# A hybrid decoder block on one core: raw weight places, retention's order and up's first sums

## The chip, the core and the metric

The kernel runs on one core of a Trainium2 chip. The core has a matrix engine (TensorE, here PE, with its weight loads as PEld), a vector engine (VectorE, DVE), a scalar engine (ScalarE, ACT), GpSimd (POOL) and SyncE (SP), which issues most transfers between the chip's memory and the core's own (SBUF). Products land in eight PSUM banks of 128 x 512 numbers. The engines run side by side, each through its own list of instructions in order, and wait for one another by semaphores. The metric is the device time of one launch in microseconds (us).

## What is computed

A decoder block over 1024 tokens of width 1024, in fp32. Cut to what matters here:

```
xn = rmsnorm(x, norm1_g)
qa, ka, va, qr, kr, vr, gr, gate_a, gate_b = split(xn @ w_in)     # w_in: 1024 x 12800
o_a = mix over three groups of dilated windowed attention (12 heads of 128, chunks of 128)
o_r = head_groupnorm(retention(qr, kr, vr)) * silu(gr)            # 4 heads, 8 chunks of 128
y = sigmoid(gate_a) * (o_a @ w_proj_a) + sigmoid(gate_b) * (o_r @ w_proj_b)
x = x + y @ w_out
x = x + square(relu(rmsnorm(x, norm2_g) @ w_up)) @ w_down         # 4096 wide
```

Retention goes over a head's chunks in order: a chunk's output is its decayed scores times its values, plus its queries times a state of 256 x 512, which each chunk then updates.

## The kernel before

**Products.** Every fp32 number is split into a high and a low half that PE takes (`split`: ACT copies the high half, DVE subtracts it). One product is then three matmuls of 128 x 512, high by high, high by low and low by high (`Pipe.group`, matmul at L271). Weights (`Weights`, called W) come as raw tiles of 128 x 1024 numbers into a few *raw places*, are split at L367 (ACT) and L370 (DVE) into places of their own, and a raw place may be loaded anew once its tile is split. Places raw0 to raw2 are there always, raw3 in a pool `more`, raw4 and raw5 in a pool `most` that is open only in some stages. Several stages use Strassen's scheme with seven products for eight: sums of weight quarters are made in the raw places by DVE (L122 for the token units, L158 for the units of up) before they are split. Pieces of a unit are named A, B, C and D, and `W` works its list of pieces in order: a piece waits for its target's earlier use to be freed, and for its raw tile.

**Stages, by time.** Norm and attention's inputs to about 400 us; then the gates, retention's queries and keys, and gr (units "in"), with attention's blocks put between its 168 steps, to about 951. Attention's three groups are mixed in four parts per pass (loads into a tile `edge`, weights L482 to L495, mix L498 and L500 on DVE, then four transposes at L506 on PE). Then the token units of retention's values (rv) to 1120; retention itself, to about 1443, laid over *fill steps* of projection a (16 of 12 matmuls) and projection b (first steps, 16 of 24 matmuls, and second steps, 8); the last second steps; out (16 rows of 24 matmuls) from about 1490; up from about 1579; down from about 1900 to 2216.

**Pools.** In the "in" stage the pools sgp (tiles `sg` for gate and gr outputs), pu0 and att lie on one stack, all closed after the stage; then `most2` opens at their place, for raw4 and raw5. So the first loads into raw4 and raw5 there come behind whatever still uses that memory, the stores `sr_d<-sg` of gr (L873) among it.

**Retention's rounds.** There are 32 items (4 heads of 8 chunks) and a round for each, plus two at the end. In round m the acts are, in this order: `turn_o(m-2)` (transposes at L1105 of the normed output `on`, scale on ACT at L1109, times the gate `sr` at L1111, split), `output(m-1)` (chunk's output, ACT copy L1068, statistics on DVE L1070 to L1072, a power on POOL L1073, norm L1075), `update(m-1)` (two products into the state, L1089 and L1091), `prepare(m)` (splits of the state into `Sh` and `Sl`) and `decay(m)` (scores L1028, mask L1030, their splits, keys turned). Acts are spread over the groups of a fill step. `share` says how many fill steps a round has: ten rounds share the 16 of projection a. Scores, output and the two updates of a round take turns in three PSUM banks, "ms".

**Projection b.** A first step puts its sum into memory (`pb_d`, tile `t`, ACT at L980); a second step loads it back (`begin`, L985 on, load at L940), ACT puts it into a PSUM bank (L992), and PE adds the second half of the terms on it.

**Out and up.** In out's second half each row is normed (sum of squares on ACT, power on POOL L384, scale on DVE L1242) and turned (`turn_xn`, L1178 to L1198), one to two rows later, with up's sums of activations made on the way. The raw tiles of up's unit 0 and 1 are loaded in out's stage; `w_out`'s last tiles use the weight places 4, 5, 2 and 3, and place 4 is up's place for piece D.

The order of PE's instructions is as written; on the other engines a scheduler sets it from the program's dependences and its own estimates.

Of the kernel before, what the change touches and what calls it, by code (L numbers as in the profile page):

```python
# [10 lines left out]
F = mybir.dt.float32  # L11
R = mybir.dt.float32r
# [25 lines left out]
class Weights:  # L38
# [93 lines left out]
    def add_units(self, tag, srcs):  # L132
# [7 lines left out]
        def piece(key, buf, r, cols, then=None, after=(), pinned=False):  # L140
            def step():
                if isinstance(buf, tuple):
                    if not kept:
                        kept["D"] = self.buffer(buf[0])
                    h, l = (x[:, 512 * buf[1]:512 * buf[1] + 512] for x in kept["D"])
                else:
                    h, l = self.buffer(buf)
                self.split(h, l, self.raw[r][:, cols], pinned)
                self.units[key] = h, l
                if then:  # L150
                    then()

            self.steps.append((self.claim(buf, key).union(after), r, step))
# [7 lines left out]
        for j in range(-1, len(srcs)):  # L161
            if j + 1 < len(srcs):
                r = base + 2 * (j + 1)
                piece((tag, j + 1, "A"), self.A[(j + 1) % 2], r, both,
                      after=((tag, j, "A"),) if j > 0 else (), pinned=tag == "up" and j > 0)
            if j >= 0:
                r = base + 2 * j
                piece((tag, j, "D"), (self.D, j % 2), r + 1, slice(0, 512), lambda r=r: sums(r))
# [149 lines left out]
def hybrid_block(ctx: ExitStack, tc: tile.TileContext, a: dict, out: bass.AP):  # L318
# [87 lines left out]
    for nb in range(2):  # L406
        for u in range(4):
            W.add(a["w_out"][nb, u], (4, 5, 2, 3)[u] if nb else (2, 3, 0, 1)[u])
# [8 lines left out]
    def product(tag, j, name, unit, operands, pu, result):  # L417
# [24 lines left out]
        elif name == "N5":  # L442
            u["u3"] = pu().tile([P, 512], F, name="u3")
            nc.scalar.activation(u["u3"], ps, AF.Copy)
        elif name == "N7":
# [300 lines left out]
    est, gates_ = ExitStack(), ExitStack()  # L746
# [3 lines left out]
    def open_gates():  # L750

        nonlocal sgp, pu, att, cmb, dist
        assert not pipe.due
        tok.close()
        W.most = None
        cmb = pool(est, "cmb", 1).tile([P, 2608], F, name="edge")
        sgp = pool(gates_, "sgp", 2)
        pu = pool(gates_, "pu0", 2)
        att = pool(gates_, "att", 2)
# [80 lines left out]
    def begins(n):  # L840
        return 3 + (n * 19) // 12
# [5 lines left out]

    def begin_mix(s, i):
        nonlocal mixing
        mixing = combine(s, i, cmb, joined.pop((s, i)))  # L850
# [7 lines left out]
    with ExitStack() as ph:  # L858

        def result(j, f, cs, src):  # L860
# [12 lines left out]
            nc.sync.dma_start(sr_d[2 * (n - NQ) + f, :, cs] if n >= NQ else rqk_d[n // 2, n % 2, f, :, cs], sg)  # L873
# [13 lines left out]
    tok = ExitStack()  # L887
    W.most = pool(tok, "most2", 1)
    W.pump()
# [42 lines left out]
    with ExitStack() as ph:  # L932
# [41 lines left out]

        def first_step(n):
            d, cs = n % KT, (lo, hi)[n // KT]
            pp = mm.tile([P, 512], F, name="mm")
            project(d, (inner, before)[n // KT], pp, True)
            t = pm2.tile([P, 512], F, name="t")
            nc.scalar.activation(t, pp, AF.Copy)  # L980
            nc.sync.dma_start(pb_d[d, :, cs], t)

        begun = {}

        def begin(n):  # L985

            if n < 2 * KT and n not in begun:
                d, cs = n % KT, (lo, hi)[n // KT]
                t = loaded(pm2, pb_d[d, :, cs], "t")
# [18 lines left out]
        share = [2, 1, 2, 1, 2, 2, 1, 2, 1, 2] + [1] * 24  # L1008
# [4 lines left out]
        def load_sr(m):  # L1013
            if m < len(ITEMS):
                h, c = ITEMS[m]
                srs[m] = p2.tile([P, 4, P], F, name="sr", bufs=3)
                nc.sync.dma_start(srs[m], sr_d[4 * h:4 * h + 4, :, c * P:(c + 1) * P].rearrange("f p t -> p f t"))

        def decay(m):
# [9 lines left out]
            sm = p2.tile([P, 2, P], F, name="sm", bufs=1)  # L1029
# [26 lines left out]
        def output(m):  # L1056
# [10 lines left out]
            on = it["o"] = p2.tile([P, DV], F, name="on")  # L1067
# [46 lines left out]
        for m in range(2):  # L1114
            load_sr(m)
        for m in range(len(ITEMS) + 2):
            acts = []
            if m >= 2:
                acts.append(lambda m=m: turn_o(m - 2))
            if 1 <= m <= len(ITEMS):  # L1120
                acts += [lambda m=m: output(m - 1), lambda m=m: update(m - 1)]
            if m < len(ITEMS):
                load_item(m + 2)
                load_sr(m + 2)
# [4 lines left out]
                acts += [lambda m=m: prepare(m), lambda m=m: decay(m)]  # L1129
# [32 lines left out]
    with ExitStack() as ph:  # L1162
# [4 lines left out]
        ssq = cp.tile([P, NT, 4], F, name="ssq")  # L1167
        kept = {}
# [4 lines left out]
        def turn_xn(xn, t, q):  # L1173

            pt = tr.tile([P, 4, P], F, name="tr")
# [320 lines left out]
```

## Time and profile before

| | |
|---|---|
| time, median of 3 runs | 2222.08 us (2219.28 to 2225.76) |
| the profiled execution | 2218.63 us |
| its span | 2216.5 us |
| PE busy | 2156.0 us, 97% |
| DVE busy | 1488.6 us, 67% |
| ACT busy | 1141.5 us, 51% |
| POOL busy | 163.6 us, 7% |
| moved by DMA | 403.28 MB, mean 182 GB/s |

The span is the time from the first to the last recorded instruction. In rows of the timeline stand the start, the length, the engine, the line, the operation, and its tiles (out<-in, numbers left out); brackets give the idle time before it and what ended it. In rows of waits stand the total idle time, its number and the longest. In rows on transfers stand the count, the KB of each, and the median time from issue to landing.

### The profile page before, as it was taken

To read this page: it belongs to the slowest core of one execution; us is meant where nothing else is said; L and a number is where in the kernel's file an instruction comes from. 1 tells how busy PE (TensorE), PEld (TensorE's weight loads), DVE (VectorE), ACT (ScalarE), POOL (GpSimd) and SP (SyncE) were. 2 spreads that over 40 slices of the span, in tenths; PEclk is the share of its full clock that TensorE was granted. 3 is DMA by queue.
4 is the path that set the end of the run, shared out by engine and by line. 5 is a ranking of instruction groups with operands and counts; after the bars stand their busy time and mean duration, and the time that the engine had idled before them with its cause. 6 is when DMAs were issued, how large, how long until landed. Compare 5 with 4: busy or idle time off the path is not lost.

```text
span 2216.5 us, 28593 instructions
## 1 busy us (share of the span) xinstructions
PE 2156.0 (97%) x9968; PEld 1770.1 (80%) x9968; DVE 1488.6 (67%) x2627; ACT 1141.5 (51%) x1990; POOL 163.6 (7%) x175
## 2 busy tenths in 40 slices
PE   8999999999999999979999999999899999999998
PEld 6888788888888887868877887888688888778887
DVE  8767676454656666656579777763877878686863
ACT  6434453577844477732246666542677777532210
POOL 1114343000000000000000000100000000000002
PEclk9999999999999999989999999999999999999999
DMA  6434434454555545444577555674378889976758
GB/s 201 129 114 115 152 85 122 152 165 138 172 155 157 174 149 158 147 138 143 171 237 224 181 162 148 175 243 140 98 222 248 248 251 281 325 280 229 258 216 176
DMA packets 336482, 403.28 MB, mean 182 GB/s; under 512 B 35345, under 2 KB 252049, under 8 KB 336338
## 3 DMA queue, kind: packets, MB, share of 16 engines
q1 hardware_dynamic: 332642, 394.38, 56.6%
q0 software_dynamic: 3696, 7.08, 2.1%
q8 instruction: 79, 1.29, 0.2%
q14 instruction: 65, 0.53, 0.1%
HBM read 262.87 MB, written 138.51 MB: 181 GB/s over the span
## 4 chain that ended last, share of the span: by engine, by line
PE 60%; issue 29%; DVE 4%; ACT 3%; DMA 3%; POOL 1%; SPq 0%; POOLq 0%; ACTq 0%; DVEq 0%
PE mm L271 30%; PE ms L271 24%; PE tr L808 1%; PE tr L827 1%; PE tr L661 1%; PE tr L820 1%; DVE wl L370 1%; PE tr L1105 1%; PE ms L1028 1%; DVE xl L370 1%; POOL out L1338 1%; DMA sr_d<-sg 0%; ACT L814 0%; ACT L868 0%; ACT wh L367 0%
## 5 line engine op out<-in xcount | busy, mean ns | idle before, releaser
L367 ACT ACTIVATE wh<-raw 128x1024 fp32r<-128x1024 f32 (+1 forms) x320 | 317.5, 994 | 320.6 <-PE ms L271 187.3
L370 DVE TENSOR_TENSOR wl<-raw,wh 128x1024 fp32r<-128x1024 f32 (+1 forms) x320 | 367.6, 1153 | 148.2 <-ACT wh L367 145.3
L271 PE MATMUL mm<-xh,wh 128*128 128x512 f32 x960 | 398.6, 415 | 5.5 <-ACT mm L992 4.0
L271 PE MATMUL mm<-xl,wh 128*128 128x512 f32 x960 | 376.4, 392 | 1.7 <-DVE xl L370 1.7
L271 PE MATMUL mm<-xh,wl 128*128 128x512 f32 x960 | 377.1, 393 | 0.5 <-DVE wl L370 0.5
L271 PEld LDWEIGHTS mm<-xh,wl 128*128 128x128 f32 x960 | 180.6, 188 | 40.4 <-DVE wl L370 1.0
L271 PEld LDWEIGHTS mm<-xh,wh 128*128 128x128 f32 x960 | 181.5, 189 | 38.9 <-ACT mm L992 4.4
L271 PE MATMUL mm<-wh,xh 128*128 128x512 f32 x528 | 208.8, 395 | 0.0
L271 PEld LDWEIGHTS mm<-xl,wh 128*128 128x128 f32 x960 | 181.6, 189 | 32.6 <-DVE xl L370 2.4
L271 PE MATMUL mm<-wh,xl 128*128 128x512 f32 x528 | 206.1, 390 | 1.5 <-DMA xl<-h_d 1.5
L271 PE MATMUL mm<-wl,xh 128*128 128x512 f32 x528 | 205.8, 390 | 0.0
L271 PE MATMUL ms<-wh,xh 128*128 128x512 f32 x512 | 205.3, 401 | 0.3 <-ACT wh L367 0.3
L271 PE MATMUL ms<-xh,wh 128*128 128x512 f32 x480 | 200.7, 418 | 0.6 <-ACT u L441 0.6
L271 PE MATMUL ms<-wl,xh 128*128 128x512 f32 x512 | 200.3, 391 | 0.9 <-DVE ss L383 0.8
L271 PE MATMUL ms<-wh,xl 128*128 128x512 f32 x512 | 200.6, 392 | 0.0
L271 PE MATMUL ms<-xl,wh 128*128 128x512 f32 x480 | 187.9, 391 | 0.7 <-DVE xl L370 0.7
L271 PE MATMUL ms<-xh,wl 128*128 128x512 f32 x480 | 188.1, 392 | 0.0
L271 PEld LDWEIGHTS mm<-wh,xl 128*128 128x128 f32 x528 | 99.3, 188 | 22.9 <-DMA xl<-h_d 1.9
L271 PEld LDWEIGHTS mm<-wh,xh 128*128 128x128 f32 x528 | 99.4, 188 | 19.7 <-ACT ms L1327 0.4
L271 PEld LDWEIGHTS mm<-wl,xh 128*128 128x128 f32 x528 | 99.4, 188 | 19.5
L271 PEld LDWEIGHTS ms<-wl,xh 128*128 128x128 f32 x512 | 96.9, 189 | 20.8 <-DVE wl L370 1.9
L271 PEld LDWEIGHTS ms<-wh,xl 128*128 128x128 f32 x512 | 96.6, 189 | 21.1
(304 smaller groups left out, 3806.5 us busy)
## 6 DMA issues: line engine op xcount, KB each, us to landing
h_d<-hs SPq DMA_DIRECT2D x112, 512.0 KB, 4.3
xh<-h_d SPq DMA_DIRECT2D x32, 896.0 KB, 4.9
xl<-h_d SPq DMA_DIRECT2D x32, 896.0 KB, 7.4
raw<-in_w_att_q SPq DMA_DIRECT2D x48, 512.0 KB, 4.5
raw<-in_w_up SPq DMA_DIRECT2D x32, 512.0 KB, 3.8
raw<-in_w_pb SPq DMA_DIRECT2D x32, 512.0 KB, 4.6
raw<-in_w_down SPq DMA_DIRECT2D x32, 512.0 KB, 4.8
qk_d<-T SPq DMA_DIRECT2D x48, 256.0 KB, 3.5
```

What stands on the lines that cost most here:

```text
L271: self.nc.tensor.matmul(ps, x, y, start=start, stop=stop, skip_group_check=not first)
L367: hi = nc.scalar.activation(dst_h, src, AF.Copy)
L370: nc.vector.tensor_tensor(dst_l, src, dst_h.bitcast(F), op=OP.subtract)
L661: nc.tensor.transpose(pt[:, i, :], c[:, i * P:(i + 1) * P], ident)
L808: nc.tensor.matmul(sp[:, :w], q[:, e * P:(e + 1) * P], k[:, k0 * P:k0 * P + w], start=True, stop=True)
L820: nc.tensor.transpose(tb[:, j * P:(j + 1) * P], st["p"][:, j * P:(j + 1) * P], ident)
L827: nc.tensor.matmul(po[:, :DH], st["t"][:, j * P:(j + 1) * P], v[:, k0 + j, :], start=(j == 0), stop=(j == nk - 1))
L1028: nc.tensor.matmul(sp[:, i * P:(i + 1) * P], key[:, f], q[:, f], start=(f == 0), stop=(f == 1))
L1105: nc.tensor.transpose(pt[:, f, :], its[m]["o"][:, f * P:(f + 1) * P], ident)
L1338: nc.gpsimd.dma_start(out[r * P:(r + 1) * P, ns], Y[r][:, ns], accum_op=OP.add)
```

## The change

Line numbers above and in the rows of the trace are those of the kernel before; in the changed kernel they are a few higher.

1. *Raw places.* The pools sgp and pu0 go to the right side of the memory. Attention's pool gets a stack of its own that closes six steps after the last block of attention begins (step 159 of 168), and `most2` opens there. The last two units of gr issue their eight stores on POOL's queue.
2. *Retention's order.* A round's acts are now `turn_o(m-3)`, `decay(m)`, `output(m-1)`, `update(m-1)`, `prepare(m)`; there is one round more at the end, and eleven rounds share the 16 steps of projection a. `on` has three buffers for two; `sr` is loaded in round m for item m-2, into two buffers for three; the mask's tile moves into `edge`.
3. *Projection b.* `begin(0)` is called ahead of the last first step, not after it; `t` has three buffers for two.
4. *Up's first sums.* `w_out`'s tile in place 4 goes to a place "o4" of its own, so that place 4 is free in out's stage for the two halves of it that hold piece D of up's units 0 and 1; a unit's sums follow its piece D. In W's list unit 1's piece A need no longer follow unit 0's, and its piece D comes when the product N5 of unit 0 is copied; the scheduler may still set what it issues ahead of that. One turn of xn2 (row 6, second half) takes an "mm" bank in place of a "tr" bank.

```diff
@@ -162,10 +163,11 @@
                 piece((tag, j + 1, "A"), self.A[(j + 1) % 2], r, both,
-                      after=((tag, j, "A"),) if j > 0 else (), pinned=tag == "up" and j > 0)
+                      after=((tag, j, "A"),) if j > 1 else (), pinned=tag == "up" and j > 1)
             if j >= 0:
                 r = base + 2 * j
-                piece((tag, j, "D"), (self.D, j % 2), r + 1, slice(0, 512), lambda r=r: sums(r))
+                piece((tag, j, "D"), (self.D, j % 2), r + 1, slice(0, 512), lambda r=r: sums(r),
+                      after=((tag, "first"),) if tag == "up" and j == 1 else ())
                 piece((tag, j, "B"), self.B[j % 2], r, both, lambda r=r: self.used.add(r))
@@ -405,7 +407,7 @@
         for u in range(4):
-            W.add(a["w_out"][nb, u], (4, 5, 2, 3)[u] if nb else (2, 3, 0, 1)[u])
+            W.add(a["w_out"][nb, u], ("o4", 5, 2, 3)[u] if nb else (2, 3, 0, 1)[u])
     NU = FF // 256
@@ -442,6 +444,8 @@
             nc.scalar.activation(u["u3"], ps, AF.Copy)
+            if j == 0:
+                W.free((tag, "first"))
         elif name == "N7":
@@ -743,20 +747,22 @@
     sgp = pu = att = cmb = dist = None
-    est, gates_ = ExitStack(), ExitStack()
+    est, gates_, heads_ = ExitStack(), ExitStack(), ExitStack()
     BLOCKS = [(slot, g, b) for slot, g in heads for b in range(NT)]
 ...
         nonlocal sgp, pu, att, cmb, dist
+        nonlocal tok
         assert not pipe.due
         tok.close()
+        tok = ExitStack()
         W.most = None
         cmb = pool(est, "cmb", 1).tile([P, 2608], F, name="edge")
-        sgp = pool(gates_, "sgp", 2)
-        pu = pool(gates_, "pu0", 2)
-        att = pool(gates_, "att", 2)
+        sgp = pool(gates_, "sgp", 2, "right")
+        pu = pool(gates_, "pu0", 2, "right")
+        att = pool(heads_, "att", 2)
         dist = att.tile([P, 2, 2 * P], F, name="dist", bufs=1)
@@ -845,6 +851,13 @@
+    def close_heads():
+        heads_.close()
+        W.most = pool(tok, "most2", 1)
+        W.pump()
+    at_slot.setdefault(begins(len(BLOCKS) - 1) + 6, []).append(close_heads)
@@ -870,7 +883,8 @@
                 nc.scalar.activation(sg, src, AF.Copy)
-            nc.sync.dma_start(sr_d[2 * (n - NQ) + f, :, cs] if n >= NQ else rqk_d[n // 2, n % 2, f, :, cs], sg)
+            queue = nc.gpsimd if n >= NQ + 6 else nc.sync
+            queue.dma_start(sr_d[2 * (n - NQ) + f, :, cs] if n >= NQ else rqk_d[n // 2, n % 2, f, :, cs], sg)
@@ -884,9 +898,6 @@
     gates_.close()
-    tok = ExitStack()
-    W.most = pool(tok, "most2", 1)
-    W.pump()
     cp = pool(tok, "cp2", 4)
@@ -972,21 +983,23 @@
+        begun = {}
 ...
             d, cs = n % KT, (lo, hi)[n // KT]
+            if n == 2 * KT - 1:
+                begin(0)
             pp = mm.tile([P, 512], F, name="mm")
             project(d, (inner, before)[n // KT], pp, True)
-            t = pm2.tile([P, 512], F, name="t")
+            t = pm2.tile([P, 512], F, name="t", bufs=3)
             nc.scalar.activation(t, pp, AF.Copy)
-        begun = {}
-
 ...
                 d, cs = n % KT, (lo, hi)[n // KT]
-                t = loaded(pm2, pb_d[d, :, cs], "t")
+                t = loaded(pm2, pb_d[d, :, cs], "t", bufs=3)
                 g = loaded(pm2, sg_d[1, d, :, cs], "s0", bufs=3)
@@ -1005,7 +1018,7 @@
                 + [lambda n=n: second_step(n) for n in range(KT)])
-        share = [2, 1, 2, 1, 2, 2, 1, 2, 1, 2] + [1] * 24
+        share = [2, 1, 2, 1, 2, 1, 2, 1, 2, 1, 1] + [1] * 24
@@ -1013,7 +1026,7 @@
                 h, c = ITEMS[m]
-                srs[m] = p2.tile([P, 4, P], F, name="sr", bufs=3)
+                srs[m] = p2.tile([P, 4, P], F, name="sr")
                 nc.sync.dma_start(srs[m], sr_d[4 * h:4 * h + 4, :, c * P:(c + 1) * P].rearrange("f p t -> p f t"))
@@ -1026,7 +1039,7 @@
                     nc.tensor.matmul(sp[:, i * P:(i + 1) * P], key[:, f], q[:, f], start=(f == 0), stop=(f == 1))
-            sm = p2.tile([P, 2, P], F, name="sm", bufs=1)
+            sm = cmb[:, 2 * S:2 * S + 2 * P].rearrange("p (a b) -> p a b", a=2)
             nc.vector.tensor_tensor(sm[:, 0], sp[:, :P], maskT[:, h, :], op=OP.mult)
@@ -1064,7 +1077,7 @@
             pipe.group(po, terms)
-            on = it["o"] = p2.tile([P, DV], F, name="on")
+            on = it["o"] = p2.tile([P, DV], F, name="on", bufs=3)
             nc.scalar.activation(on, po, AF.Copy)
@@ -1111,22 +1124,23 @@
-        for m in range(2):
-            load_sr(m)
-        for m in range(len(ITEMS) + 2):
+        for m in range(len(ITEMS) + 3):
             acts = []
-            if m >= 2:
-                acts.append(lambda m=m: turn_o(m - 2))
-            if 1 <= m <= len(ITEMS):
-                acts += [lambda m=m: output(m - 1), lambda m=m: update(m - 1)]
+            if m >= 3:
+                acts.append(lambda m=m: turn_o(m - 3))
             if m < len(ITEMS):
                 load_item(m + 2)
-                load_sr(m + 2)
                 q, k = (ring[m % 4][:, 256 * i:256 * i + 256].rearrange("p (f t) -> p f t", f=2) for i in range(2))
 ...
                 split(*it["v"], ring[m % 4][:, 512:])
-                acts += [lambda m=m: prepare(m), lambda m=m: decay(m)]
+                acts.append(lambda m=m: decay(m))
+            if 2 <= m < len(ITEMS) + 2:
+                load_sr(m - 2)
+            if 1 <= m <= len(ITEMS):
+                acts += [lambda m=m: output(m - 1), lambda m=m: update(m - 1)]
+            if m < len(ITEMS):
+                acts.append(lambda m=m: prepare(m))
             if share[m] == 2:
@@ -1165,6 +1179,8 @@
         ssq = cp.tile([P, NT, 4], F, name="ssq")
+        W.places["o4"] = [cp.tile([P, UW], R, name=f"o4{i}") for i in "hl"]
+        W.free(("place", "o4"))
         kept = {}
@@ -1172,7 +1188,10 @@
-            pt = tr.tile([P, 4, P], F, name="tr")
+            if q and t == 6:
+                pt = mm.tile([P, 512], F, name="mm").rearrange("p (a b) -> p a b", b=P)
+            else:
+                pt = tr.tile([P, 4, P], F, name="tr")
             for i in range(4):
 ...
                 nc.tensor.transpose(pt[:, i, :], xn[:, k * P:(k + 1) * P], ident)
```

On SP's queue, at the end of the "in" stage, before (L217 loads raw tiles of rv, L467 loads the mix's pieces, L873 stores gr):

```order
L873 DMA sr_d_84<-sg_8526 128x512
L467 DMA edge_3538<-acc_d_80 128x3x130 x4
L873 DMA sr_d_84<-sg_8557 128x512
L217 DMA raw2_8713<-in_w_rv_q 128x1024
L873 DMA sr_d_84<-sg_8573 128x512
L873 DMA sr_d_84<-sg_8597 128x512
L217 DMA raw3_8723<-in_w_rv_q 128x1024
L873 DMA sr_d_84<-sg_8658 128x512
L873 DMA sr_d_84<-sg_8682 128x512
L873 DMA sr_d_84<-sg_8701 128x512
L217 DMA raw4_8711<-in_w_rv_q 128x1024
L217 DMA raw5_8721<-in_w_rv_q 128x1024
```

And now (L219 loads raw tiles, L837 stores attention's outputs, L471 loads the mix's pieces, L513 stores a mix):

```order
L837 DMA acc_d_80<-acc_8226 128x2x130
L219 DMA raw4_8540<-in_w_rv_q 128x1024
L471 DMA edge_3538<-acc_d_80 128x3x130
L219 DMA raw2_8477<-in_w_rv_q 128x1024
L471 DMA edge_3538<-acc_d_80 128x3x130 x3
L219 DMA raw5_8593<-in_w_rv_q 128x1024
L219 DMA raw3_8538<-in_w_rv_q 128x1024
L219 DMA raw2_8591<-in_w_rv_q 128x1024
L219 DMA raw3_8676<-in_w_rv_q 128x1024
L513 DMA oa_d_81<-edge_3538 128x512
```

The load into raw4 has moved to the place behind attention's last store, the one into raw5 in between the mix's loads, and gr's last eight stores are no more on this queue.

On ACT, at the last first step of projection b, before (L980 copies the step's sum out, L992 puts a loaded sum into a bank, L1109 begins a turn):

```order
L367 ACTIVATE vh_12729<-edge_3538 128x512
L367 ACTIVATE Sh_12470<-St0_11698 128x512 x2
L1051 ACTIVATE kzh_12495<-tr_12492,rc_101 128x256
L367 ACTIVATE wh5_12502<-raw0_12173 128x1024
L367 ACTIVATE smh_12484<-sm_12482 128x128
L980 ACTIVATE t_12508<-mm_12409 128x512
L992 ACTIVATE mm_12524<-t_12520 128x512
L992 ACTIVATE mm_12530<-t_12526 128x512
L992 ACTIVATE mm_12638<-t_12634 128x512
L1109 ACTIVATE onT_12543<-tr_12538,gng_102 128x128 x4
```

And now (L995, L1005 and L1122 are the same three):

```order
L1081 ACTIVATE on_12387<-ms_12377 128x512
L369 ACTIVATE vh_12640<-edge_3538 128x512
L369 ACTIVATE Sh_12412<-St0_11647 128x512 x2
L369 ACTIVATE wh2_12421<-raw2_12095 128x1024
L995 ACTIVATE t_12427<-mm_12329 128x512
L1005 ACTIVATE mm_12443<-t_12439 128x512
L1122 ACTIVATE onT_12457<-tr_12452,gng_102 128x128 x4
L369 ACTIVATE smh_12472<-edge_3538 128x128
L369 ACTIVATE xh_9846<-onT_12457 128x4x128
L1053 ACTIVATE qh_12591<-ring1_9855 128x256
```

One L1005 stands here where three L992 stood, and a turn follows it; the load it waits for is issued one fill step sooner.

On DVE, at up's first sums, before (L158 sums of unit 0, in raw0 and raw1; wl4 piece D of unit 0 and unit 1; L1242 norm of a row):

```order
L370 TENSOR_TENSOR wl4_14301<-raw1_13892,wh4_14300 128x512
L1238 TENSOR_TENSOR ssq_13652<-ssq_13652 128x1
L158 TENSOR_TENSOR raw1_13892<-raw1_13892 128x512
L383 TENSOR_SCALAR ssq_13652<-ssq_13652 128x1
L370 TENSOR_TENSOR wl4_14301<-raw3_13896,wh4_14300 128x512
L1242 SCALAR_TENSOR_TENSOR xn2_14290<-y0_14175,ssq_13652,g2_13650 128x512
L1242 SCALAR_TENSOR_TENSOR xn2_14290<-xr_14173,ssq_13652,g2_13650 128x512
L158 TENSOR_TENSOR raw1_13892<-raw1_13892,raw0_13890 128x512
L370 TENSOR_TENSOR xl_92<-x0_14316,xh_91 128x4x128
L158 TENSOR_TENSOR raw0_13890<-raw0_13890,raw1_13892 128x512
L370 TENSOR_TENSOR xl_94<-x1_14334,xh_93 128x4x128
L158 TENSOR_TENSOR raw0_13890<-raw0_13890 128x512
```

And now (L159 sums of unit 0 and of unit 1, in raw2 and raw3; L1261 the norm, of the first row of out's second half):

```order
L159 TENSOR_TENSOR raw3_13864<-raw3_13864,raw2_13862 128x512
L372 TENSOR_TENSOR wl1_13883<-raw2_13862,wh1_13882 128x1024
L159 TENSOR_TENSOR raw1_13860<-raw1_13860,raw0_13858 128x512
L372 TENSOR_TENSOR wl0_13873<-raw0_13858,wh0_13872 128x1024
L1253 TENSOR_TENSOR xr_13833<-mm_13901,xr_13833 128x512
L159 TENSOR_TENSOR raw0_13858<-raw0_13858,raw1_13860 128x512
L159 TENSOR_TENSOR raw2_13862<-raw2_13862,raw3_13864 128x512
L159 TENSOR_TENSOR raw0_13858<-raw0_13858 128x512
L1257 TENSOR_TENSOR ssq_13610<-ssq_13610 128x1
L159 TENSOR_TENSOR raw2_13862<-raw2_13862 128x512
L385 TENSOR_SCALAR ssq_13610<-ssq_13610 128x1
L1261 SCALAR_TENSOR_TENSOR xn2_13932<-y0_13835,ssq_13610,g2_13608 128x512
```

The sums stood among the norms and turns of the last rows; now those of both units stand ahead of the first row's norm.

## The prediction

> **What bounds the kernel now.** First I read the page's busy times, then the table of what TensorE (PE) waited for.
>
> ```profile
> span 2216.5 us, 28593 instructions
> PE 2156.0 (97%) x9968; PEld 1770.1 (80%) x9968; DVE 1488.6 (67%) x2627; ACT 1141.5 (51%) x1990; POOL 163.6 (7%) x175
> ```
>
> PE is busy 97% of the span and the change adds and removes no PE instruction. So only two things can be won: the 2216.5 − 2156.0 = 60.5 us not busy, and what the clock loses behind long waits. The table of waits gives idle time, count and longest wait:
>
> ```profile
> PE tr L506 <- DVE edge L500: 14.2, 3, 12.9
> ...
> PE tr L1105 <- DVE on L1075: 4.3, 3, 1.7
> PE mm L271 <- ACT mm L992: 4.0, 1, 4.0
> PE tr L1178 <- DVE x L1198: 2.8, 1, 2.8
> ...
> PE mm L271 <- DVE xl L370: 1.7, 1, 1.7
> ...
> PE mm L271 <- ACT wh L367: 1.5, 1, 1.5
> ```
>
> The change touches four of these places. I call them **B** (L506, the mix at the start of values), **C** (L1105, retention's turns), **D** (L992, the first loaded sum of projection b) and **E** (the other three rows, 2.8 + 1.7 + 1.5 = 6.0 us, and one more of 0.7 that is shown below: 6.7 us, where out meets up). The next rows show the clock behind B and behind D (columns: stretch and its length; PE, PEld, DVE, ACT, POOL busy; granted clock; DMA share; GB/s).
>
> ```profile
> 973.00:977.00 4.00, 3.86 (x10) 3.10 (x11) 0.09 (x1) 1.20 (x2) 0.00 (x0) 0.54 0.17 66
> 1367.30:1374.40 7.10, 7.10 (x22) 5.73 (x23) 0.69 (x1) 2.77 (x7) 0.00 (x0) 0.62 0.62 210
> ```
>
> Busy time hides this cost: (1 − 0.54) × 4.0 = 1.8 us behind B, and (1 − 0.62) × 7.1 = 2.7 us behind D.
>
> **B: raw places open earlier.** The timeline, all engines:
>
> ```profile
> 948.32 0.33 SPq L217 DMA_DIRECT2D raw<-in_w_rv_q  x1
> 949.90 4.68 SPq L873 DMA_DIRECT2D sr_d<-sg  x3
> 958.04 0.81 SPq L217 DMA_DIRECT2D raw<-in_w_rv_q  x2
> 958.88 0.38 PE L506 MATMUL tr<-ident,edge 128*128 128x128 f32 x2
> 961.72 4.75 DVE L122 TENSOR_TENSOR raw<-raw,raw 128x1024 f32<-128x1024 f32 x4 [7.49 <-DMA raw<-in_w_rv_q]
> 972.17 0.48 PE L506 MATMUL tr<-ident,edge 128*128 128x128 f32 x1 [12.91 <-DVE edge L500]
> ```
>
> Loads into raw4 and raw5 are issued only behind the last stores of gr, at 958.04. DVE idles 7.49 us for them, then does six sums (L122) and two splits, and only then the mix that PE's next transposes need. PE stands from 958.88 to 972.17; wait and clock cost 12.9 + 1.8 = 14.7 us.
>
> After the change both loads are issued among the mix's own loads. The late load that remains goes to raw3, at the place of the one at 948.32. These rows price it and the stores moved to POOL:
>
> ```profile
> raw<-in_w_rv_q SPq DMA_DIRECT2D x24, 512.0 KB, 4.3
> sr_d<-sg SPq DMA_DIRECT2D x32, 256.0 KB, 2.5
> s<-sg_d POOLq DMA_DIRECT2D x3, 256.0 KB, 3.1
> 1078.34 0.78 POOL L940 DMA_DIRECT2D s<-sg_d  x1 [697.62 <-DVE wl L370]
> ```
>
> It lands near 948.3 + 4.3 = 952.6. Ahead of the third mix split DVE then has one sum (4.75 / 4 = 1.2), a product for gr, two splits, one more sum and small pieces, some 7 us: ready at about 960, and the fourth about 1 us behind. PE arrives at 958.88, so about 2 us of stall are left. Eight stores go to POOL, at 0.8 us of issue and 3.1 us to land where SP's take 2.5: up to 1.4 us later each. Behind them on POOL stands nothing until 1078 (idle 697.62 us); who waits is ACT, for its two gr buffers, and through one product DVE: half a microsecond of the 2 us above. Bounds: 0 left (saves 14.7) and 5 left with its clock loss of about 2 (saves 8). I take **13**.
>
> *Weighed against the Trainium skill.* "DMA: Bandwidth & Descriptors", section "SWDGE vs HWDGE vs iDMA", would send plain transfers to SP or ACT and says that GpSimd's descriptor writes can be held up by DVE. It speaks against these eight stores. The rows above agree in sign (3.1 against 2.5) but show no holding up; by the rule the stall at B would end nearer 5 us than 2. The sum goes by the rows.
>
> **C: retention's order.** C lies in the stage of projection a, 16 short fill steps that carry ten rounds of retention. First most of that stage, then a part of the stage behind it, then DVE's large groups in the first (busy, mean ns, idle before).
>
> ```profile
> 1134.00:1205.60 71.60, 68.24 (x331) 55.23 (x332) 62.83 (x135) 44.17 (x96) 4.21 (x7) 1.00 0.76 237
> 1205.60:1300.00 94.40, 94.40 (x466) 78.56 (x465) 72.71 (x155) 61.27 (x128) 5.51 (x10) 1.00 0.59 184
> L966 DVE TENSOR_TENSOR s<-s,mm 128x512 f32<-128x512 f32 x12 | 8.1, 676 | 0.0
> ...
> L370 DVE TENSOR_TENSOR wl<-raw,wh 128x1024 fp32r<-128x1024 f32 (+1 forms) x6 | 6.7, 1123 | 0.0
> ...
> L1111 DVE TENSOR_TENSOR onT<-onT,sr 128x512 f32<-128x512 f32 x8 | 5.5, 688 | 2.0 <-ACT onT L1109 2.0
> L370 DVE TENSOR_TENSOR xl<-onT,xh 128x512 fp32r<-128x512 f32 x8 | 5.5, 684 | 0.9 <-ACT xh L367 0.7
> ```
>
> A round's turn waits for `on` of the round before; turned three rounds back it has a whole round, 7 to 10 us, more, which is over the longest wait of 1.7. Against this the stage now holds 11 rounds for 10. DVE's load of one, without its turn, is (62.83 − 8.1 − 6.7 − 5.5 − 5.5) / 8 = 4.6 us, so DVE goes from 62.8 of 71.6 us to 67.4 of about 73 (3 us of stalls less, some 4 of PE's work more, which only changes stage): still under the end, but at 92% it will be late here and there, for `Sl` and for the PSUM banks above all. Bounds: 4.3 saved and a loss of 2. I take **3**.
>
> **D: begin(0) one step earlier.**
>
> ```profile
> 1363.34 0.42 SPq L940 DMA_DIRECT2D t<-pb_d  x1
> 1366.60 0.60 ACT L992 ACTIVATE mm<-t 128x512 f32<-128x512 f32 x1 [1.81 <-DMA t<-pb_d]
> 1367.25 0.80 PE L271 MATMUL mm<-xh,wh 128*128 128x512 f32 x1 [4.01 <-ACT mm L992]
> ```
>
> The load is issued at 1363.34, just as PE needs the sum it carries, and PE resumes 3.9 us later. Issued at the start of the last first step, 24 matmuls sooner, it has some 5 us for those 3.9. ACT's copy now stands ahead of the turn's copies in ACT's order and may wait some 2 us for the landing; the turn behind it has that slack (stage behind C: PE 94.40 of 94.40). Wait and clock, 4.0 + 2.7 = 6.7, go; bounds 4 and 6.7. I take **6**.
>
> **E: up's first sums in out's stage.** Windows of out, then of the crunch; DVE's sums in it; a wait on POOL's power; PE's last waits there:
>
> ```profile
> 1490.00:1530.00 40.00, 40.00 (x178) 33.11 (x177) 7.99 (x10) 7.32 (x17) 0.00 (x0) 1.00 0.45 150
> 1573.40:1600.30 26.90, 21.69 (x104) 16.79 (x103) 26.13 (x45) 15.78 (x27) 1.48 (x2) 1.00 0.24 79
> L158 DVE TENSOR_TENSOR raw<-raw,raw 128x512 f32<-128x512 f32 x3 | 2.1, 684 | 0.0
> 1578.00 0.75 DVE L1242 SCALAR_TENSOR_TENSOR xn<-y,ssq,g 128x512 f32<-128x512 f32 x1 [0.44 <-POOL ssq L384]
> 1597.76 0.50 PE L271 MATMUL ms<-xl,wh 128*128 128x512 f32 x1 [0.67 <-DVE xl L370]
> 1604.77 0.50 PE L271 MATMUL mm<-xh,wh 128*128 128x512 f32 x1 [1.49 <-ACT wh L367]
> ```
>
> Here DVE is the bound: 26.13 of 26.90. Out's stage, where DVE is busy 7.99 of 40, takes six of its sums and two half splits at some 0.6 us each, 8 × 0.6 = 4.8, and gives back one full split of unit 1 (1.1). Of those 3.7, about 1.5 are lost to three waits of 0.44 that the sums used to fill. PE then reaches 1597.76's matmul 2.2 us sooner. The wait of 1.5 behind it goes too, with a smaller one on the low half, since unit 2's first split no longer stands behind unit 1's sums. 2.2 + 1.5 and that smaller one make **4**; bounds 6 and 1. Nothing else pays for the sums: out's loads and place "o4" are hidden under 40.00 of 40.00 PE.
>
> *Weighed against the Trainium skill.* E's stalls flow together into one of about 3.5 us (2.8 + 1.7 + 0.7 and a few small ones, less 2.2). "TensorE: Matmul & The Clock Gate", section "Part 1: The HAM clock gate", has the clock halved after an idle window of about 3.4 us; the trace agrees so far, with 0.54 and 0.62 after 12.9 and 4.0 us, and 1.00 in the stretch with the 2.8. By that rule a merged stall could cost E about 2 more.
>
> The sum: 13 + 3 + 6 + 4 = **26 us**.
>
> **The rivals.**
>
> 1. *DVE only passes its waits on.* In C and E the same work stands closer together; PE waits for `Sl` in place of `on`, and in E for the last xl at the same time as before. Against it: 2.2 us of E is less work in a full engine. C and E then give 0, and 13 + 6 = 19 are saved.
> 2. *The early opening does not hold.* raw5 or raw3 lands as late as before, because the loads wait for the release of attention's memory or for the stores on POOL. Then B keeps its stall, and 3 + 6 + 4 = 13 are saved. Against it: in SP's order raw4's load stands right behind attention's last store, where seven stores of gr stood between the two.
> 3. *All four go wholly*: 14.7 + 4.3 + 6.7 + 6.7 = 32 saved.
> 4. *Slower.* Retention has three banks for four products a round; now the decay product's bank passes to the second product of update, where before the output's did. In the old order DVE's mask product follows its matmuls by 2.1 us:
>
> ```profile
> 1217.64 0.60 PE L1028 MATMUL ms<-ring 128*128 128x128 f32 x4
> 1219.78 0.29 DVE L1030 TENSOR_TENSOR sm<-ms,maskT 128x128 f32<-128x128 f32 x1
> ```
>
> In a round of one fill step the new order leaves some 17 matmuls, at 94.40 / 466 = 0.20 us each 3.4 us, before the bank is wanted: 1 more than the 2.4 at which the product ends here. Were DVE later by w + 1 us in each of the 20 rounds with an update, PE would wait 20 w. The gain is gone at w = 1.3; slower by more than the 6.7 us (0.3%) that can be told from no change needs w over 1.6, say 2: 40 − 26 = 14 us slower. For it speaks DVE's 77% in the stage behind C; against it that PE waits there nowhere.
>
> **How the numbers follow.** The profiled execution took 2218.63 us, 2.1 over its span; the median of the three shown is 2222.08, 3.4 above it. From the median the forecast gives 2222.1 − 26 = 2196, from the profiled one 2192.6. I say 2195, nearer to the median. Chances: forecast (saved 22 to 30) 0.54, rival 1 (2203) 0.22, rival 2 (2209) 0.09, rival 3 (2190) 0.05, rival 4 slower (2236) 0.04, and its mild form, w of 1 to 1.6, no change, 0.06. So faster 0.90, same 0.06, slower 0.04. The range, 2185 to 2209, runs from rival 3 on the profiled time to rivals 1 and 2, and leaves out rival 4 and some of the edges.
>
> **What would show it.** B: the L506 row of the waits falls from 14.2 to under 4, the clock in the 4 us behind it is 1.00, and raw loads stand among the mix's loads. C: L1105's row vanishes; a row of `Sl` or a bank in its place is rival 1 or 4. D: no wait for the ACT copy of pb, clock 1.00 behind it. E: DVE's sums stand before the first xn, one wait of 2 to 4 us on xl is left, and those behind it are gone. The prediction is wrong if PE's idle time falls by less than 15 us, or if the clock falls behind a merged stall.

## The result

The changed kernel takes **2191.74 us** (median of 4 runs, 2190.48 to 2193.37) against 2221.4 us of the kernel before (4 runs, 2219.28 to 2225.76) on the same chip. The ratio is 0.9864, 95% interval 0.9847 to 0.9882: 29.7 us less. The forecast was 2195, in a range of 2185 to 2209.

The page and the waits of PE in the changed kernel, in the same form as those shown of before:

```profile
span 2191.6 us, 28596 instructions
PE 2153.8 (98%) x9968; PEld 1769.8 (81%) x9968; DVE 1487.0 (68%) x2627; ACT 1139.9 (52%) x1990; POOL 170.0 (8%) x183
```

```profile
PE tr L665 <- POOL ss L386: 2.6, 1, 2.6
PE ms L273 <- ACT xh L369: 2.5, 1, 2.5
PE mm L273 <- DMA xl<-h_d: 2.1, 1, 2.1
...
PE tr L510 <- DVE edge L504: 1.2, 2, 0.8
...
PE ms L273 <- DVE xl L372: 0.7, 1, 0.7
PE ms L273 <- DVE Sl L372: 0.6, 2, 0.4
```

What PE does not do fell from 60.5 to 2191.6 − 2153.8 = 37.8 us. The 12.9 us on the mix are gone, L510 (L506 before) has 1.2 us in two waits. The turns' wait on `on` and the one on ACT's copy of projection b have no row any more. At E one wait of 2.5 us on ACT's `xh` is left, with 0.7 behind it.

PE issues 9968 matmuls in both kernels, so the starts of the n-th of each (counted from 0) can be set side by side. Only retention's are in another order, so C and D can't be parted sharply this way.

| instruction of PE | before, us | changed, us | difference | gained since the row above |
|---|---|---|---|---|
| first | 4.32 | 4.19 | −0.1 | |
| 4250, end of attention | 908.09 | 910.62 | +2.5 | −2.7 |
| 5000, after B | 1091.30 | 1078.76 | −12.5 | **15.1** (B) |
| 6750, after C and D | 1466.68 | 1442.53 | −24.2 | **11.6** (C, D) |
| 7250, in out | 1575.82 | 1551.83 | −24.0 | −0.2 |
| 7500, after E | 1639.26 | 1612.27 | −27.0 | **3.0** (E) |
| 8500, end of up | 1865.93 | 1838.94 | −27.0 | 0.0 |
| last | 2208.61 | 2183.99 | −24.6 | −2.4 |

The four places give 15.1 + 11.6 + 3.0 = 29.7 us, as much as the medians differ. This one execution shows 5 us less, which it lost at two places that the change leaves alone (the last section). A second profile of the changed kernel (the run changed_again below) gives 15.0, 12.0 and 3.0 at the four places and 28.4 us in all.

B in the changed kernel, all engines' rows that matter, then the clock behind it:

```profile
950.97 0.33 SPq L219 DMA_DIRECT2D raw<-in_w_rv_q  x1
954.62 1.22 DVE L122 TENSOR_TENSOR raw<-raw,raw 128x1024 f32<-128x1024 f32 x1
960.51 0.73 DVE L504 SCALAR_TENSOR_TENSOR edge<-edge 128x128 f32<-128x128 f32 x2
961.41 0.49 PE L510 MATMUL tr<-ident,edge 128*128 128x128 f32 x3
962.26 0.33 PE L510 MATMUL tr<-ident,edge 128*128 128x128 f32 x1 [0.36 <-DVE edge L504]
```

```profile
962.30:966.30 4.00, 4.00 (x18) 3.33 (x19) 0.50 (x1) 2.50 (x4) 0.00 (x0) 1.00 0.17 66
1122.00:1190.00 68.00, 67.80 (x336) 55.92 (x335) 62.11 (x135) 42.42 (x93) 3.95 (x8) 1.00 0.82 256
1346.00:1354.00 8.00, 8.00 (x43) 6.69 (x42) 6.94 (x15) 6.10 (x13) 0.86 (x1) 1.00 0.48 162
1571.70:1579.70 8.00, 7.97 (x28) 6.38 (x29) 3.60 (x5) 4.88 (x9) 0.00 (x0) 0.79 0.33 90
```

PE's third transpose waits for nothing, the fourth 0.36 us. The second fence has B, most of C, D and the stretch behind E: clock 1.00 in the first three, PE busy in 67.80 of 68.00 us of C with DVE at 91%, and at E a clock of 0.79 behind the merged wait.

### The profile page after: what moved, and what is told of

It reads as the page before. It is cut to its first block, busy times and chain, and to the rows that moved or that the text cites. A ratio compares the mean times of both kernels' runs of the same rounds, so it can differ in the third digit from the quotient of the medians.

```text
span 2191.6 us, 28596 instructions
## 1 busy us (share of the span) xinstructions
PE 2153.8 (98%) x9968; PEld 1769.8 (81%) x9968; DVE 1487.0 (68%) x2627; ACT 1139.9 (52%) x1990; POOL 170.0 (8%) x183
## 4 chain that ended last, share of the span: by engine, by line
PE 55%; issue 30%; DVE 6%; ACT 3%; DMA 3%; POOL 1%; SPq 0%; POOLq 0%; ACTq 0%; DVEq 0%
PE mm L273 28%; PE ms L273 22%; PE tr L814 1%; DVE wl L372 1%; PE tr L833 1%; PE tr L665 1%; ACT wh L369 1%; DMA sg_d<-sg 1%; PE ms L1041 1%; PE tr L826 1%; DMA sr_d<-sg 1%; DVE xl L372 1%; DVE raw L159 1%; POOL out L1357 1%; PE tr L1118 0%
## 5 line engine op out<-in xcount | busy, mean ns | idle before, releaser
L273 PEld LDWEIGHTS mm<-wh,xl 128*128 128x128 f32 x520 | 97.7, 188 | 23.2 <-DMA xl<-h_d 2.5
```

Source lines behind the costliest of these rows:

```text
L273: self.nc.tensor.matmul(ps, x, y, start=start, stop=stop, skip_group_check=not first)
```

## The experiments

Each undoes one part of the changed kernel or does one apart, and is compared with the changed kernel: by medians, and by the table's method in the stage that it touches (for retention, matmuls 5000 to 6750). The scatter of single executions, about 2 us, blurs the stages little: the two profiles of the changed kernel differ by 0.4 us in retention's stage and by less than 0.1 at B and E. Medians are less sure: the kernel before came out at 2220.1, 2221.2 and 2222.3 us beside these runs, and the changed kernel once more at 1.8 us less than at first, so 2 us between two medians tell little by themselves.

**The four parts, one undone at a time.**

The first closes the pools together again and puts all stores on SP:

```diff
-        sgp = pool(gates_, "sgp", 2, "right")
-        pu = pool(gates_, "pu0", 2, "right")
-        att = pool(heads_, "att", 2)
+        sgp = pool(gates_, "sgp", 2)
+        pu = pool(gates_, "pu0", 2)
+        att = pool(gates_, "att", 2)
...
+    tok = ExitStack()
+    W.most = pool(tok, "most2", 1)
+    W.pump()
```

> The changed kernel with its first part undone: the pools of the gates' outputs and of attention close together again, raw4 and raw5 open behind them, and all of gr's stores are on SP's queue. Theory (the parts add, and this one is worth the 13.4 us of waits and 1.8 us of clock at B): 15 us slower than the changed kernel, about 2207; the L510 wait of about 13 us is back, with the clock near 0.54 in the 4 us behind it, and nothing else differs. Rival (B's gain was partly given back by the 2.5 us that the changed kernel loses ahead of 951, through the stores on POOL or the earlier loads): 12 to 13 us slower, about 2204, and PE reaches the first product of the values 2 us or more earlier than in the changed kernel's trace.

Measured: 2207.93 us (2207.72 to 2210.85), 16.2 slower; 15.8 in the stage.

```profile
PE tr L510 <- DVE edge L504: 14.6, 3, 13.2
...
PE ms L273 <- DVE edge L1036: 1.3, 2, 1.1
```

The wait is back whole, so part one alone carries B. The early opening gives nothing back ahead of 951: at matmul 4250 this kernel is 1.8 us ahead of the changed one's profile, but the next three runs, with the opening in place, are 2.1 to 2.9 ahead. The second row is the bank wait of the prediction's fourth rival: it exists, in two rounds, 1.3 us.

The second puts back retention's old steps, turns two rounds on, ten rounds over projection a:

> The changed kernel with the second part undone but for the mask's place: turns two rounds back, the steps in the old order, ten rounds over projection a's 16 steps. Theory (the new order removes the waits of the turns, and every other stall of this stage with them): 5 to 6 us slower than the changed kernel, about 2197; waits of about 4 us on the normed output are back. Rival (half of the 5.6 us between the two traces comes from the third part, which starts its copy sooner): 3 us slower, about 2195.

Measured: 2200.49 us (2198.19 to 2202.33), 8.8 slower; 8.6 in the stage, more than either theory gave.

```profile
PE tr L1118 <- DVE on L1088: 4.7, 4, 1.9
...
PE ms L273 <- DVE sml L372: 1.4, 2, 1.3
```

The turns' waits are back, 4.7 us. The second row is new: at the place of D, near 1355, PE now waits for the scores' split.

The third calls `begin(0)` behind the last first step, with two buffers for `t` again:

```diff
-            if n == 2 * KT - 1:
-                begin(0)
...
```

> The changed kernel with the third part undone: the first loaded sum of projection b is asked for behind the last first step. Theory (the wait was the load's way through memory, and its clock loss): 6 to 6.7 us slower than the changed kernel, about 2198; a wait of about 4 us on the ACT copy is back, clock about 0.6 in the 7 us behind. Rival (the new order of retention alone would have moved the copy ahead far enough): 1 us or less slower, about 2192.

Measured: 2192.51 us (2190.08 to 2193.55), 0.8 slower; 4.1 at the place itself (between matmuls 6300 and 6325), 4.4 in the whole stage.

```profile
1350.21 0.80 PE L273 MATMUL mm<-xh,wh 128*128 128x512 f32 x1 [2.30 <-ACT mm L1003]
```

```profile
1350.20:1358.20 8.00, 7.99 (x34) 6.68 (x35) 1.77 (x4) 2.40 (x6) 0.00 (x0) 0.79 0.57 192
```

```profile
1574.00:1582.00 8.00, 7.94 (x35) 6.59 (x36) 3.64 (x6) 4.77 (x9) 0.00 (x0) 1.00 0.33 89
```

The wait is back at 2.3 us, not 4.0, and costs 2.3 + (1 − 0.79) × 8 = 4.0. By the median nearly nothing is lost (2.5 us against the changed kernel's second median, below). The trace shows where its own execution got it back: 2.1 ahead of the end of attention, 1.7 at E, where the clock held (1.00 in the last row) behind the same wait of 2.5 us, and 2.2 in down, where a wait was 1.35 us and not 2.1, with no clock lost behind it. The 4.1 at the place is the better reading of part three; that it is worth as much in the median is not shown.

The fourth puts w_out's tile in place 4 again, with the sums among the last norms:

> The changed kernel with the fourth part undone: w_out's tile is in place 4 again, the sums of up's first two units stand among the last norms, and the turn takes its tr bank. Theory (DVE is the bound of the last 27 us of out; the change took 3.7 us of its work away, but the clock fell behind the merged wait of 2.5 us): 3 us slower than the changed kernel, about 2195, and where the clock holds in the changed kernel too 4 to 5. Rival (what is left at E is set by the chain of norms and turns alone): within 1 us of the changed kernel, 2192.

Measured: 2194.45 us (2191.6 to 2200.53), 2.7 slower; 3.0 in the stage.

```profile
PE tr L1189 <- DVE x L1209: 2.8, 1, 2.8
PE mm L272 <- DVE xl L371: 1.7, 1, 1.7
...
PE mm L272 <- ACT wh L368: 1.2, 1, 1.2
```

The three old waits are back. The stage confirms the theory; the medians, whose runs overlap, can't tell. E takes as long as in the kernel before (63.4 us from matmul 7250 to 7500), though the clock over the 8 us behind the wait of 2.8 is 0.79 here and 1.00 there: what PE loses in speed here, it waits less further on.

**Part three without part two.** Undoing gave 8.6 for part two and 4.1 to 4.4 for part three, some 13 together, where both gained 11.6. So part three was done alone, on the kernel before:

> The kernel before with the third part alone (and the mask's place moved, for memory). Theory (part three takes the 4.0 us wait and its 2.4 us of clock away, but PE comes to retention's next steps that much sooner and waits there some 2.4 us in small pieces, as it did in the run with retention undone): about 4 us faster than the kernel before, about 2217. Rival (the wait's gain comes whole): 6.5 us faster, about 2214.5; or, as the median of the run without it said, it gains nothing: 2221.

Measured: 2219.15 us (2216.56 to 2222.9) against 2222.3; ratio 0.9989 (0.9979 to 0.9999). In the stage it gains 2.7 us, 1.8 of them at D: by matmul 6300 it has gained 4.5 there, by 6325 it has lost 2.6 of them. Near 1370 the same small waits come in the place of D's, and the clock falls behind them:

```profile
1370.00:1378.00 8.00, 7.46 (x26) 5.96 (x27) 5.20 (x13) 3.72 (x9) 0.55 (x1) 0.79 0.69 223
```

So the theory's mechanism held, with a clock loss of about 1.7 us that it had not counted. Of the 11.6 us part two brings 7.2 by itself (the run undo_begin against the kernel before, in the stage), part three 2 to 3 (this run; 3.0 in undo_retention against the kernel before), and the last 1 to 2 only come when both are there.

**The halves of part two.** Old steps, but turns three rounds back:

```diff
-                acts.append(lambda m=m: decay(m))
...
-                acts.append(lambda m=m: prepare(m))
+                acts += [lambda m=m: prepare(m), lambda m=m: decay(m)]
```

> The changed kernel with retention's steps in the old order (output, update, prepare, decay) but turns still three rounds back and eleven rounds over projection a. Tells which half of the second part pays. Theory (the turns' waits for the normed output were 4.3 of the 4.8 us, and with a round more they are gone; decay's place matters for the two small waits on the split scores alone): within 1 us of the changed kernel, about 2192, L1118's waits absent. Rival (decay ahead of output is what keeps PE from waiting for the scores' splits when DVE carries eleven rounds): 3 us or more slower, with waits on the scores' halves (smh, sml) in many rounds.

New steps, but turns two rounds back (ten rounds share the 16 steps of projection a again, and `sr` is loaded one round ahead):

```diff
-            if m >= 3:
-                acts.append(lambda m=m: turn_o(m - 3))
+            if m >= 2:
+                acts.append(lambda m=m: turn_o(m - 2))
...
```

> The changed kernel with retention's steps in the new order but turns two rounds back, ten rounds over projection a, the gate loaded one round ahead. Theory (the turn's distance pays): about 4 us slower than the changed kernel, about 2196, with waits of about 4 us on the normed output (L1117) between 1115 and 1190, and in the stretch of the last rounds near 1350 1 to 2 us more. Rival (the order pays): within 1 us, about 2192.

Measured: 2197.7 us (2196.94 to 2199.42), 6.0 slower, and 2223.37 us (2220.06 to 2226.73), 31.6 slower; in the stage 8.8 and 31.8. Their waits, in this order, with most of projection a's stage for the first:

```profile
PE ms L273 <- ACT smh L369: 4.2, 5, 1.6
...
PE ms L273 <- DVE sml L372: 2.0, 4, 0.9
```

```profile
1122.00:1190.00 68.00, 65.37 (x324) 53.29 (x322) 61.07 (x129) 43.51 (x92) 5.87 (x8) 1.00 0.77 241
```

```profile
PE tr L1118 <- DVE on L1088: 23.2, 20, 3.2
```

Both theories fell: of the first run the rival held, the second has the sign right and the size wrong by a factor of eight. Each half needs the other; in the stage the later turn alone gains nothing (8.8 lost, against 8.6 with both halves undone). With decay last in a round, its scores are split too late for the next round's output, now that eleven rounds share the stage: 6.2 us of waits on their halves. With decay first, output comes later in its round, and a turn two rounds back meets an unfinished `on` in 20 rounds, 23.2 us. The later turn is what makes the new order possible, and the new order is what keeps the splits ahead.

**The queue of gr's last stores.** All on SP again, all else as changed:

```diff
-            queue = nc.gpsimd if n >= NQ + 6 else nc.sync
-            queue.dma_start(sr_d[2 * (n - NQ) + f, :, cs] if n >= NQ else rqk_d[n // 2, n % 2, f, :, cs], sg)
+            nc.sync.dma_start(sr_d[2 * (n - NQ) + f, :, cs] if n >= NQ else rqk_d[n // 2, n % 2, f, :, cs], sg)
```

> The changed kernel with gr's last eight stores back on SP's queue; everything else as changed. Theory (the wait at B was the memory of raw4 and raw5; the queue does not matter, since the loads stand ahead of the stores they used to follow, and a store that waits for its product on SP is at most one product ahead of the next load): the same within 1.5 us, about 2192, the waits at the mix of the values (L510) under 1.5 us in all. Rival (SP's queue in order would hold the last load behind a store that is not ready, so that POOL's queue is what makes the opening work): the L510 wait is 3 us or more, and the time 2195 or more.

Measured: 2190.78 us (2188.37 to 2191.64), 1.0 less than the changed kernel, with overlapping runs. The wait at B is 0.38 us in this kernel, 0.36 in the changed one. The queue pays nothing: theory confirmed. The Trainium skill ("DMA: Bandwidth & Descriptors", "SWDGE vs HWDGE vs iDMA") gives plain transfers to SP or ACT; following that costs nothing here, and breaking it did not cost the 3 us that the prediction set beside it.

**What is left at E.** The turns of out's last four rows split N6's operand first, its sum in a tile of its own:

```diff
-            put(OP7["N3"], cut, pt)
-            nc.vector.tensor_tensor(x2, x2, pt, op=OP.subtract)
-            nc.vector.tensor_tensor(pt, x3, pt, op=OP.add)
-            put(OP7["N6"], cut, pt)
+            x6 = pn.tile([P, 4, P], F, name="x6", bufs=1)
+            nc.vector.tensor_tensor(x6, x3, pt, op=OP.add)
+            put(OP7["N6"], cut, x6)
+            nc.vector.tensor_tensor(x2, x2, pt, op=OP.subtract)
             put(OP7["N5"], cut, x3)
+            put(OP7["N3"], cut, pt)
             put(OP7["N7"], cut, x2)
-            nc.vector.tensor_tensor(x1, x1, pt, op=OP.subtract)
+            nc.vector.tensor_tensor(x1, x1, x6, op=OP.subtract)
```

> The changed kernel with the turns of out's last four rows in another order: the sum for N6 goes into a tile of its own and is split first, then the others. In the changed kernel PE waits 2.52 us for the last of these splits, with 0.67 behind it, and lost about 1.7 us of clock there. Theory (DVE's list ahead of N6's split is what sets that wait; two DVE operations of 0.6 us each leave it): the wait falls to about 1.3 us, no clock is lost behind it, the time is 1.5 to 3 us shorter, about 2189 to 2190. Rival (ACT's list or the norm's chain sets it): the wait stays over 2 us and the time is the same within 1 us.

Measured: **2186.72 us** (2185.32 to 2189.46), ratio to the kernel before 0.9847 (0.9832 to 0.9862), the fastest of all. The stage gains 2.9 us.

```profile
1566.74 0.50 PE L273 MATMUL ms<-xh,wh 128*128 128x512 f32 x1 [1.66 <-ACT xh L369]
1567.56 0.50 PE L273 MATMUL ms<-xl,wh 128*128 128x512 f32 x1 [0.32 <-DVE xl L372]
```

```profile
1567.60:1575.60 8.00, 8.00 (x36) 6.64 (x37) 5.34 (x8) 4.74 (x10) 0.00 (x0) 1.00 0.10 29
```

The wait falls by 0.86, not by the 1.2 of two operations; the one behind it by 0.35; and the clock behind it is 1.00 in place of 0.79, worth 1.7. The stage confirms the theory's 1.5 to 3 us, with the size of the wait a little off (1.66 for 1.3); the median fell further than the 2189 to 2190 expected.

Both last edits together, beside the changed kernel once more:

> The changed kernel with N6's operand first in the turns (as in the run n6_first) and gr's last stores on SP's queue. Theory (the queue is worth nothing either way, the order of the turns about 3 us): 2186 to 2189, within 1.5 us of n6_first, L510's waits under 1.5 us. Rival (the queue on SP gains 1 us of itself): 2185.5 or less.

> The changed kernel itself, once more, beside the next run on the same chip. Theory (a wait of PE of 2.0 to 3.2 us costs about 1.7 us of clock behind it in some executions and nothing in others, so single executions scatter by some us): the median within 1 us of 2191.7, the same waits of 2.5 us where out meets up and of about 2 us in down, but not the same clocks behind them as in the first profile. Rival (the clock behind a wait is fixed by the program): the clock is near 0.79 again behind the waits at 227, 1571 and 1886 and 1.00 behind the one at 1931.

Measured: 2188.34 us (2187.17 to 2190.41), and 2189.98 us (2188.17 to 2190.04) for the changed kernel, 1.8 under its first median. The rival of n6_first_sp falls: the queue gains nothing beside n6_first either. By these two medians the turns' order, with the queue, is worth 1.6 us, by the two medians of the changed kernel against n6_first 3 to 5; the stage's 2.9 lies between. In the changed kernel's second profile the waits at E (2.55 us) and in down (2.08 and 2.05) came again with the same clocks behind them, 0.79, 0.79 and 1.00. There the theory missed and the rival held; the wait at 227 was 1.76 and not 2.56, so it says nothing on that place.

## Why the prediction was right, and where not

- **The place of the gain was right**: idle time at B, C, D and E and the clock behind B and D. 29.7 us came for 26 forecast, 2191.7 for 2195. Most of the missing 4 us is in B and in C with D.
- **B, 13 forecast, 15.1 measured.** The mechanism was right, the leftover was mis-sized, 2 us for 0.36. The prediction counted 11.7 us from the issue of the last raw load to the third mix split (948.3 to about 960); the trace has 961.24 − 950.97 = 10.3, against 10.4 us until PE is there (961.41). The load was used 3.65 us after its issue, not 4.3, and stores on POOL held nothing up. The gain is over the bound of 14.7, which counted only the longest of the three waits at L506 (12.9 of 14.2 us).
- **C, 3 forecast, and D, 6 forecast: 9 for 11.6.** Both went wholly, which the prediction gave to its third rival. C's term took DVE's load right (92% forecast, 91% measured) but drew the wrong conclusion: that DVE at 92% would be late for `Sl`. It was late by 0.6 us in two waits. DVE at 91% is no wait when what PE needs next is early in its list, and the new order does just that: with the old order in old_order_turn3 DVE is 90% busy in the same stretch, and PE idles 2.6 us of 68 where it idles 0.2. The turn's distance alone, which the prediction named as the reason, gains nothing in the stage.
- **D's 6 us were set down to part three alone.** By itself it brings 2 to 3 us, since the splits of the scores are late next, at the same place, and part two without it already takes D's wait from 4.0 to 2.3. The prediction looked for what is late next behind D only on ACT.
- **E, 4 forecast, 3.0 measured.** The waits fell a little more than forecast, into one of 2.5 with 0.7 behind it (the sum had 3.5), and those further on went. What the sum left out is the clock: 0.79 over 8 us, 1.7 us lost. In the run undo_begin, where the clock held behind the same wait, E gains 4.7. The prediction had set about 2 us beside its sum for this. The Trainium skill ("TensorE: Matmul & The Clock Gate", "Part 1: The HAM clock gate") has the clock halved after an idle window of about 3.4 us; here it fell behind a wait of 2.5 us, and the measurement decides. Whether it falls behind such a wait is luck (the last section).
- **The signs of being wrong.** Of the two that the prediction named last, one came: the clock fell behind a merged stall, and that part of E's account failed. PE's idle time fell by 60.5 − 37.8 = 22.7 us, well over the 15 of the other.
- **The rivals.** The first fell: DVE did not pass its waits on. The second fell with B. The third, all gone, promised 2 us too much, by E's clock and last wait. The fourth, a bank that waits for DVE's mask product, is real but costs at most 1.4 us in one or two rounds (1.4 in stores_on_sp, 1.3 with the places undone, nothing in the changed kernel), not 1.3 in each of 20.

## What to carry to other kernels

A stall that ends on one engine's list is moved by putting what is needed next early in that list; how full the engine is decides less than what stands ahead. Two edits at one wait should be tried apart and together: here each half of the reordering alone was 6 to 32 us worse than both, and the edit that looked like the whole cause of D's gain was worth about a third of it by itself. When memory, not a queue, holds a load back, move the memory: once it was free, the queue made no difference. What the other queue would do with the memory as it was is not shown.

## What was not expected of the hardware

A wait of PE of 2.0 to 3.2 us sometimes costs clock behind it and sometimes not. The wait at 227 shows it best: the instructions ahead of it are the same in all kernels. It was 2.55 to 2.56 us in five profiles; the granted clock of the 8 us behind it is, of the kernel before, the changed one, and the runs undo_places, only_begin and n6_first:

```profile
227.00:235.00 8.00, 8.00 (x42) 6.70 (x42) 7.90 (x12) 5.83 (x14) 7.58 (x5) 1.00 0.35 131
```

```profile
226.80:234.80 8.00, 7.97 (x32) 6.48 (x33) 6.81 (x10) 5.11 (x11) 6.87 (x5) 0.79 0.17 62
```

```profile
226.90:234.90 8.00, 8.00 (x32) 6.44 (x33) 6.81 (x10) 5.07 (x11) 6.93 (x5) 0.79 0.17 64
```

```profile
226.70:234.70 8.00, 8.00 (x32) 6.49 (x33) 6.89 (x10) 5.19 (x11) 7.11 (x5) 0.79 0.17 63
```

```profile
227.60:235.60 8.00, 8.00 (x42) 6.70 (x43) 7.90 (x12) 5.81 (x14) 7.58 (x5) 1.00 0.35 131
```

At 0.79 PE does 10 matmuls fewer in those 8 us, and its later starts slip by 1.6 us against those of the kernel before. Behind waits of 3.19 and 2.83 us in the run new_order_turn2 the clock was 1.00, behind 2.00 us in undo_begin 0.79.

The traces show what decides: where the wait falls. In each profile the stretches at the lower clock begin on one grid with steps of 3.413 us. But for the one at the end of the span they last whole steps, at a clock of 0.50, which makes 0.79 over 8 us. In the kernel before they begin at 963.06, 1365.83 and 1956.34 us, 118 and 173 steps apart. Below are the steps that hold the wait at 227: two of the kernel before, then one of the changed kernel and the step behind it.

```profile
222.39:225.80 3.41, 2.05 (x10) 1.35 (x8) 3.41 (x5) 1.14 (x4) 0.44 (x2) 1.00 0.73 195
225.80:229.22 3.42, 2.22 (x12) 1.94 (x13) 2.59 (x5) 2.08 (x6) 3.18 (x3) 1.00 0.10 38
```

```profile
224.48:227.90 3.42, 1.07 (x7) 1.01 (x8) 2.59 (x6) 1.58 (x5) 2.44 (x3) 1.00 0.31 119
227.90:231.31 3.41, 3.41 (x10) 2.63 (x9) 3.27 (x5) 1.55 (x4) 3.23 (x3) 0.50 0.00 0
```

In the kernel before the grid cuts the wait in two, PE is idle for 1.36 and 1.20 us of the steps, and the clock holds. In the changed kernel 2.35 us of it lie in one step, and the next step runs at 0.50. Between the first and the last matmul of all thirteen profiles, each of the 26 steps at full clock with 2.0 us of idle time or more is followed by a step at 0.50, 3 of the 21 with 1.6 to 2.0 us are, and none of the 90 with 1.0 to 1.6. The grid begins elsewhere in every run. So whether a wait of 2.0 to 3.2 us costs 1.7 us of clock or none is luck, and that the places at E and in down came out alike in both profiles of the changed kernel was luck too. Two or three such waits in an execution can make the scatter of some 2 us that a median of four does not fully take out.

The other loss ahead of B, about 1 us of the 2.7, lies in attention's small waits. In the changed kernel's second profile the whole loss is absent: it is 0.4 us ahead of the kernel before at matmul 4250.
